# The Griffin block's two input projections as three fp32r products each, in a two-layer decoder trunk

## The chip, the core and the metric

The kernel runs on one core of one Trainium2 chip, in one launch. The metric is device time in microseconds (us), the median over several executions. One execution was also taken by the hardware profiler; its rows are shown below.

## The reference

The input x has 256 tokens (rows) of 1024 features, in float32. Two layers follow each other.

- Layer 0: RMSNorm, an input projection 1024 to 2560, a convolution branch and an attention branch, an output projection, residual add.
- Layer 1, whose mixer the change touches:

```python
def mixer_c(h, w_in, conv_w, conv_b, w_r, b_r, w_i, b_i, lam, w_out):
    u = h @ w_in
    gate, xr = jnp.split(u, 2, axis=-1)
    xr = causal_depthwise_conv(xr, conv_w) + conv_b
    y = rg_lru(xr, w_r, b_r, w_i, b_i, lam) * jax.nn.gelu(gate)
    return y @ w_out
```

  Here `w_in` is 1024 by 2048, the convolution has width 4, and `rg_lru` makes two gates r and i as sigmoids of `xr @ w_r` and `xr @ w_i` (eight blocks of 128x128 each) and runs the recurrence h_t = a_t h_(t-1) + sqrt(1 - a_t^2) i_t x_t with a = exp(-8 r softplus(-lam)).
- After each mixer: RMSNorm, then a squared-ReLU MLP (1024 to 4096 to 1024), residual add. At the end a last RMSNorm.

## The kernel before, in words

Everything stays in on-chip memory except the weights, which stream in once. Activations are held transposed: a tile has 128 features on the partitions and the 256 tokens along the free axis, so 1024 features are eight tiles `xT0` to `xT7`. A projection of one block of 128 outputs is eight matmuls (k = 0 to 7) that add up in one PSUM bank, with a 128x128 block of weights as the stationary operand and a 128x256 tile of x as the moving one. There are eight banks: `bank_a` 0 to 3 and `bank_b` 0 to 3; the projections rotate through the b banks, so the fourth one after a given one needs that one's bank read out.

**Two kinds of product.** A matmul of plain float32 operands ("whole") is one instruction in the program, which the profile records as two MATMUL rows. The MLPs instead *split* both operands into a high part, rounded to the type fp32r, and a low part, the rest, and make high*high + high*low + low*high. For the MLP's up projection `project_wide` (line 675) puts high and low of x side by side as one moving operand of 512 columns; its down projection uses three matmuls of 256 columns (`out_mm`, line 934).

**Weights.** A *piece* is 1 MB of weights, loaded by two DMAs of 512 KB on the SP queue, in the order in which `piece` (line 507) was called; a piece holds two *units* of 128 outputs each (128 rows of weights each, for the output projections). A piece lands in one of five `raw` buffers, used in rotation. `weights(u)` (line 554) splits a unit into a `wh`/`wl` pair, also in rotation, of which there are eight: for each half of the unit a cast to `wh` (on ScalarE or VectorE) and a subtraction into `wl` (on VectorE), each on 128x512 elements. From the sixth in a row on, a piece whose units stay whole lands straight in a pair (one unit in `wh`, one in `wl`), which then holds no split weights. SP issues strictly in order, and a DMA waits until its buffer has been read for the last time.

**The second mixer** (lines 1033 to 1134), with c = 0 to 7 for the blocks of 128 channels: `xr_proj(c)` projects, `xr_tail(c)` scales by `rstd` (the norm's factor, which `finish_norm` makes with one matmul of `ssum` against ones, a square root on ScalarE and a reciprocal on VectorE) and runs the width-4 convolution on VectorE; `gates(c)` makes two whole matmuls with the blocks of `w_r` and `w_i` (the piece called "ri") and two sigmoids; `recur_a`, `recur_b`, `recur_c` make the recurrence; `gate_chunk(c)` projects the gate branch, `gate_out(c)` applies GELU and multiplies. Then the output projection: `out_rows` for the first four blocks, `out_cols` for the others. The x tiles for the mixer come from `residual_chunk` (line 699), called while the first MLP's `out_cols` finishes.

**Order.** The program records all operations first, and a planner (class `Plan`) then simulates them with a table of costs and writes each engine's instructions in the order it found; matmuls keep almost the program's order. All engines run their own queue in order, and so an instruction that waits holds up those behind it. Almost all instructions carry line 310, where the planner emits them; tile names tell them apart.

Of the kernel before, what the change touches and what calls it, by code (L numbers as in the profile page):

```python
# [326 lines left out]
def hybrid_trunk(ctx, tc, x, mix_norm, mlp_norm, w_up, w_down, ab_w_in, ab_conv_w, ab_ln_g, ab_ln_b,  # L327
# [87 lines left out]
    def mms(items, after=()):  # L415

        calls, outs, ins, c = [], [], [], 0.0
        for o, l, r, st, sp in items:
            calls.append(("matmul", (o,), {"lhsT": l, "rhs": r, "start": st, "stop": sp, "skip_group_check": True}))
            outs.append(o)  # L420
            ins += [l, r]
            c += max(fsize(r) / 2400.0, 0.0533) * (1 if l.dtype == F32R else 4) + (0.0135 if l.dtype == F32R else 0.005)
        return plan.add("T", calls, outs[:1], ins, {"T": c}, after=after)
# [75 lines left out]

    pieces, units = [], []
    homes, pairs = [], {}
    turn = {"raw": 0, "pair": 0, "whole": 0}

    def piece(kind, ap, whole=True):
        n = len(pieces)
        pieces.append((kind, ap))
        us = [len(units), len(units) + 1]  # L510
        units.extend([(n, 0), (n, 1)])
        turn["whole"] = turn["whole"] + 1 if whole else 0
        if turn["whole"] > NRAW:
            i = turn["pair"] % NSPL
            turn["pair"] += 1
            homes.append((whs[i], wls[i]))
        else:
            raw = raws[turn["raw"] % NRAW]
            turn["raw"] += 1
            homes.append((raw[:, :1024], raw[:, 1024:]))  # L520
        if not whole:
            for u in us:
                pairs[u] = turn["pair"] % NSPL
                turn["pair"] += 1
        return us

    def cols(w, c, whole=True):

        return piece("c", w.rearrange("(k p) c -> p k c", p=P)[:, :, c * P:(c + 2) * P], whole)

    def rows(ap, whole=True):
        return piece("r", ap, whole)

    taken = [0, 0]
    got = {}
# [51 lines left out]
    for us in (((u_gate, 4), (u_val, 0)), ((u_q, 8), (u_k, 12))):  # L587
        for c in (0, 2):
            for u, at in us:
                u += cols(w_in, at + c)  # L590
    u_v = rows(wv[:, 0:4]) + rows(wv[:, 4:8])
    wo = ab_w_out[0].rearrange("(k p) c -> p k c", p=P)
    u_o = {}
    for k in (4, 6, 0, 2):
        u_o[k], u_o[k + 1] = rows(wo[:, k:k + 2])
    LAG, TAIL = 4, 4

    def mlp_units(layer):
        up, dn = [], []
        wd = w_down[layer].rearrange("(f p) c -> p f c", p=P)  # L600
        for f in range(0, NF + LAG, 2):
            if f < NF:
                up += cols(w_up[layer], f, False)
            if f >= LAG:
                dn += rows(wd[:, f - LAG:f - LAG + 2], False)
        return up, dn

    u_up, u_dn, u_xr, u_gt, u_co = {}, {}, [], [], []
    u_up[0], u_dn[0] = mlp_units(0)
    for c in range(0, 8, 2):  # L610
        u_xr += cols(c_w_in[0], 8 + c)
        if c == 2:
            u_r, u_i = piece("ri", None)
    for c in range(0, 8, 2):
        u_gt += cols(c_w_in[0], c)
    wco = c_w_out[0].rearrange("(k p) c -> p k c", p=P)
    for k in range(0, 8, 2):
        u_co += rows(wco[:, k:k + 2])
    u_up[1], u_dn[1] = mlp_units(1)


# [45 lines left out]
    def par(name, c):  # L667
        i = col0[name] + c
        return pcol[:, i:i + 1]


    def project(dst, u, xs):
        w = weights(u)
        for k in range(KD):
            mms([(dst, w[k], xs[k], k == 0, k == KD - 1)])

    def project_wide(b, u, xs):

# [19 lines left out]

    def residual_chunk(k, acc, gname, g0, xs):
        tt(xT[k], acc, xT[k], OP.add)  # L700
        g = par(gname, g0 + k)
        xs[k] = scaled(xT[k], g) if gname == "mix" else split_act(xT[k], g, "x", KD)
        if k in (0, KD - 2):
            act(ssum if k == 0 else sumb, xT[k], AF.Square)
        else:
            sq = rot("nsq", 2)
            act(sq, xT[k], AF.Square)
            if k < KD - 2:
                tt(ssum, ssum, sq, OP.add)
            else:  # L710
                tt(sumb, sumb, sq, OP.add)
# [219 lines left out]
        t = [bank("a") for _ in range(4)]  # L931
        return [t[c // 2][:, (c % 2) * S:(c % 2 + 1) * S] for c in range(KD)]

    def out_mm(acc, c, w, xp, start, stop):
        if not isinstance(w, tuple):
            return mms([(acc, w[c], xp, start, stop)])
        mms([(acc, a[:, c, :], b, start and n == 0, stop and n == 2)
             for n, (a, b) in enumerate(((w[0], xp[0]), (w[0], xp[1]), (w[1], xp[0])))])

    def out_rows(accs, u, xp, first):  # L940
        w = weights(u)
        for c in range(KD):
            out_mm(accs[c], c, w, xp, first and c % 2 == 0, False)

    def out_cols(accs, us, xps, done):
        ws = [weights(u) for u in us]
        for c0 in range(0, KD, 2):
            for c in (c0, c0 + 1):
                for i, (w, xp) in enumerate(zip(ws, xps)):
                    out_mm(accs[c], c, w, xp, False, i == len(us) - 1)  # L950
            done(c0)
            done(c0 + 1)

# [269 lines left out]
```

## Time and profile before

| what | us |
|---|---|
| median of 3 runs (588.99 to 589.18) | 589.08 |
| the profiled execution | 588.62 |
| its span, first to last instruction | 586.8 |
| TensorE (PE) busy | 579.9 |
| VectorE (DVE) busy | 413.1 |
| ScalarE (ACT) busy | 289.7 |

The profiled execution takes 1.8 us more than its span. In the rows below, a line gives the start, the length, the engine, then output<-inputs by the program's names without buffer numbers, the shape, and how many instructions were merged into the line; in square brackets, how long the engine sat idle before it and who ended that. Lengths of merged or pipelined instructions overlap, so the cost of one is read from the distance between starts. Matmul ends are modelled.

### The profile page before, as it was taken

How to read it: one execution, taken by the hardware profiler on the slowest of the kernel's cores; microseconds unless marked ns; L12 is line 12 of the kernel's file. 1: busy time of each engine (PE TensorE's matmuls, PEld its weight loads, DVE VectorE, ACT ScalarE, POOL GpSimd, SP SyncE). 2: the span in 40 equal slices, each digit the busy share in tenths (PEclk: the TensorE clock that was granted, in tenths of full speed). 3: DMA queues.
4: the chain of work that ended last, by engine and by line, in shares of the span. 5: the costliest groups of instructions: out<-in, count | busy, mean ns of one | idle time of the engine just before them, and what ended most of it. 6: DMA issues, size and time to landing. Idle time of an engine off the chain costs nothing.

```text
span 586.8 us, 9026 instructions
## 1 busy us (share of the span) xinstructions
PE 579.9 (99%) x3305; PEld 510.2 (87%) x3305; DVE 413.1 (70%) x946; ACT 289.7 (49%) x592; POOL 2.8 (0%) x22
## 2 busy tenths in 40 slices
PE   9999999999999999999999999999999999999995
PEld 8888768889999999999998888888888888888885
DVE  2599998599777767677446777559876767767732
ACT  4131435467554555555321798327555555545523
POOL 1000000000000000000000000000000000000000
PEclk9999999999999999999999999999999999999999
DMA  7997704125664665566677005924645664563001
GB/s 222 324 382 256 258 1 144 71 70 163 203 212 145 191 217 166 166 205 203 218 223 280 1 0 157 370 83 143 196 164 180 196 198 144 185 212 107 1 1 72
DMA packets 67612, 98.74 MB, mean 168 GB/s; under 512 B 3212, under 2 KB 55664, under 8 KB 67568
## 3 DMA queue, kind: packets, MB, share of 16 engines
q1 hardware_dynamic: 67568, 98.17, 50.7%
q8 instruction: 26, 0.43, 0.3%
q14 instruction: 18, 0.15, 0.1%
HBM read 97.11 MB, written 1.05 MB: 167 GB/s over the span
## 4 chain that ended last, share of the span: by engine, by line
PE 99%; ACT 0%; DVE 0%; issue 0%; ACTq 0%
PE bank_b L310 56%; PE bank_a L310 42%; ACT arena L395 0%; DVE arena L310 0%; ACT arena L310 0%; DVE ones L310 0%; DVE tiny L310 0%; DVE eps L310 0%; ACTq L310 0%
## 5 line engine op out<-in xcount | busy, mean ns | idle before, releaser
L310 DVE TENSOR_TENSOR wl<-raw,wh 128x512 fp32r<-128x512 f32 x256 | 175.1, 690 | 84.5 <-ACT wh L395 76.3
L395 ACT ACTIVATE wh<-raw 128x512 fp32r<-128x512 f32 x223 | 139.5, 630 | 168.2 <-PE bank_b L310 104.3
L310 PE MATMUL bank_b<-x,wh 128*128 128x512 f32 x512 | 184.7, 401 | 0.0
L310 PE MATMUL bank_b<-x,wl 128*128 128x256 f32 x512 | 143.8, 281 | 0.0
L310 PEld LDWEIGHTS bank_b<-x,wh 128*128 128x128 f32 x512 | 96.4, 188 | 20.9
L310 PEld LDWEIGHTS bank_b<-x,wl 128*128 128x128 f32 x512 | 96.8, 189 | 0.1
L310 PE MATMUL bank_a<-f,wh 128*128 128x256 f32 x512 | 93.2, 283 | 0.0
L310 PEld LDWEIGHTS bank_a<-f,wh 128*128 128x128 f32 x512 | 79.6, 191 | 1.4
L310 PE MATMUL bank_a<-f,wl 128*128 128x256 f32 x256 | 72.4, 283 | 0.0
L310 PE MATMUL bank_a<-wh,f 128*128 128x512 f32 (+1 forms) x256 | 72.2, 364 | 0.0
L310 PE MATMUL bank_b<-xg,raw 128*128 128x256 f32 x288 | 64.1, 379 | 0.0
L310 PEld LDWEIGHTS bank_b<-xg,raw 128*128 128x128 f32 x288 | 54.1, 190 | 7.3
L310 PEld LDWEIGHTS bank_a<-wh,f 128*128 128x128 f32 x256 | 45.9, 188 | 9.1
L310 DVE SCALAR_TENSOR_TENSOR arena<-arena,wcol 128x256 f32<-128x256 f32 x120 | 49.5, 478 | 0.0
L310 PEld LDWEIGHTS bank_a<-f,wl 128*128 128x128 f32 x256 | 49.0, 192 | 0.0
L310 PE MATMUL bank_a<-wl,f 128*128 128x512 f32 (+1 forms) x128 | 46.5, 363 | 0.0
L310 PE MATMUL bank_a<-arena,wh 128*128 128x256 f32 x128 | 34.4, 381 | 0.0
L310 PE MATMUL bank_a<-arena,wl 128*128 128x256 f32 x128 | 33.9, 379 | 0.0
L310 DVE TENSOR_TENSOR relu<-bank_b,relu 128x256 f32<-128x256 f32 x64 | 26.7, 417 | 10.1 <-ACT relu L310 10.1
L310 ACT ACT_TABLE_LOAD x24 | 30.8, 1283 | 3.0 <-PE bank_b L310 1.9
L310 ACT ACTIVATE relu<-relu 128x256 f32<-128x256 f32 x64 | 26.1, 411 | 8.2 <-DVE relu L310 5.1
L310 ACT ACTIVATE relu<-bank_b 128x256 f32<-128x256 f32 x64 | 23.6, 369 | 11.6 <-PE bank_b L310 11.6
(125 smaller groups left out, 594.3 us busy)
## 6 DMA issues: line engine op xcount, KB each, us to landing
raw<-in_w_up_dram SPq DMA_DIRECT2D x64, 512.0 KB, 5.7
raw<-in_w_down_dram SPq DMA_DIRECT2D x64, 512.0 KB, 4.8
raw<-in_c_w_in_dram SPq DMA_DIRECT2D x8, 512.0 KB, 5.4
raw<-in_ab_w_in_dram SPq DMA_DIRECT2D x6, 512.0 KB, 7.8
wh<-in_ab_w_in_dram SPq DMA_DIRECT2D x5, 512.0 KB, 8.7
wl<-in_ab_w_in_dram SPq DMA_DIRECT2D x5, 512.0 KB, 8.8
raw<-in_ab_w_in_dram SPq DMA_DIRECT2D x8, 256.0 KB, 5.7
wh<-in_ab_w_out_dram SPq DMA_DIRECT2D x4, 512.0 KB, 10.0
```

What stands on the lines that cost most here:

```text
L310: r.append(getattr(self.engines[o.eng], method)(*map(sub, a), **{n: sub(v) for n, v in k.items()}))
L395: return e.activation(sub(out), sub(a), AF.Copy, **({"scale": scale} if ap else {}))
```

## The change

Each call that declares a piece now says where it goes: "raw", "pair" or "split". The units of `c_w_in` (eight for the `xr` half, eight for the gate half) become "split"; the piece "ri" and the output projection's pieces are "pair". A common function `mm` makes one matmul or three, and `project` uses it (three of 256 columns each; not `project_wide`). `residual_chunk` splits x for the mixer as it does for the MLPs. The gates' matmuls and the output projection stay whole.

```diff
-    def piece(kind, ap, whole=True):
+    def piece(kind, ap, place):
...
-        turn["whole"] = turn["whole"] + 1 if whole else 0
-        if turn["whole"] > NRAW:
+        if place == "pair":
             i = turn["pair"] % NSPL
             turn["pair"] += 1
             homes.append((whs[i], wls[i]))
...
     for c in range(0, 8, 2):
-        u_xr += cols(c_w_in[0], 8 + c)
+        u_xr += cols(c_w_in[0], 8 + c, "split")
         if c == 2:
-            u_r, u_i = piece("ri", None)
+            u_r, u_i = piece("ri", None, "pair")
     for c in range(0, 8, 2):
-        u_gt += cols(c_w_in[0], c)
+        u_gt += cols(c_w_in[0], c, "split")
...
-        u_co += rows(wco[:, k:k + 2])
+        u_co += rows(wco[:, k:k + 2], "pair")
...
+    def mm(dst, w, k, x, first, last):
+
+        ps = ((w[0][:, k], x[0]), (w[0][:, k], x[1]), (w[1][:, k], x[0])) if isinstance(w, tuple) else ((w[k], x),)
+        mms([(dst, a, b, first and n == 0, last and n == len(ps) - 1) for n, (a, b) in enumerate(ps)])
+
     def project(dst, u, xs):
         w = weights(u)
         for k in range(KD):
-            mms([(dst, w[k], xs[k], k == 0, k == KD - 1)])
+            mm(dst, w, k, xs[k], k == 0, k == KD - 1)
...
-        g = par(gname, g0 + k)
-        xs[k] = scaled(xT[k], g) if gname == "mix" else split_act(xT[k], g, "x", KD)
+        xs[k] = split_act(xT[k], par(gname, g0 + k), "x", KD)
```

On PE, at the second `xr` projection of layer 1, before the change (`xg` are the scaled whole x tiles, `raw_73` holds units 0 and 1; the row with `ssum` is the norm's matmul):

```order
L310 MATMUL bank_b_109<-xg_123,raw_73 128x256
L310 MATMUL bank_b_109<-xg_124,raw_73 128x256
L310 MATMUL bank_b_110<-ssum,ones 128x256
L310 MATMUL bank_b_109<-xg_125,raw_73 128x256
L310 MATMUL bank_b_109<-xg_126,raw_73 128x256
L310 MATMUL bank_b_111<-xg_119,raw_74 128x256
```

The same place on PE after it (`x_129` to `x_136` are the split tiles of x):

```order
L310 MATMUL bank_b_108<-x_136,wh_1_509 128x256 x2
L310 MATMUL bank_b_108<-x_136,wl_1_643 128x256
L310 MATMUL bank_b_109<-x_129,wh_1_528 128x256 x2
L310 MATMUL bank_b_109<-x_129,wl_1_661 128x256
L310 MATMUL bank_b_109<-x_130,wh_1_528 128x256 x2
L310 MATMUL bank_b_109<-x_130,wl_1_661 128x256
L310 MATMUL bank_b_110<-ssum,ones 128x256
L310 MATMUL bank_b_109<-x_131,wh_1_528 128x256 x2
```

Each whole matmul became three, and the norm's matmul stands after two steps of the second projection where it stood after six.

On SP, the loads of layer 1's mixer before the change (the first digit of a name is the buffer: `wh5` is the high half of pair 5):

```order
L310 DMA raw4_75<-in_c_w_i_dram 128x8x128
L310 DMA raw0_71<-in_c_w_in_dram 128x4x256 x2
L310 DMA raw1_72<-in_c_w_in_dram 128x4x256 x2
L310 DMA wh1_2_2499<-in_c_w_in_dram 128x4x256
L310 DMA wl1_2_2505<-in_c_w_in_dram 128x4x256
L310 DMA wh2_2_2546<-in_c_w_in_dram 128x4x256
L310 DMA wl2_2_2552<-in_c_w_in_dram 128x4x256
L310 DMA wh3_2_2559<-in_c_w_in_dram 128x4x256
L310 DMA wl3_2_2568<-in_c_w_in_dram 128x4x256
L310 DMA wh4_2_2587<-in_c_w_in_dram 128x4x256
L310 DMA wl4_2_2592<-in_c_w_in_dram 128x4x256
L310 DMA wh5_2_2700<-in_c_w_out_dram 128x1024
```

And after it, from the first piece of `c_w_in` on:

```order
L310 DMA raw2_73<-in_c_w_in_dram 128x4x256 x2
L310 DMA raw3_74<-in_c_w_in_dram 128x4x256 x2
L310 DMA wh5_2_2699<-in_c_w_r_dram 128x8x128
L310 DMA wl5_2_2705<-in_c_w_i_dram 128x8x128
L310 DMA raw4_75<-in_c_w_in_dram 128x4x256 x2
L310 DMA raw0_71<-in_c_w_in_dram 128x4x256 x2
L310 DMA raw1_72<-in_c_w_in_dram 128x4x256 x2
L310 DMA raw2_73<-in_c_w_in_dram 128x4x256 x2
L310 DMA raw3_74<-in_c_w_in_dram 128x4x256 x2
L310 DMA raw4_75<-in_c_w_in_dram 128x4x256 x2
L310 DMA wh2_2_3053<-in_c_w_out_dram 128x1024
```

The piece "ri" moved from a raw buffer into pair 5, the pair in which the output projection's first piece landed; six of the eight pieces of `c_w_in` now stand behind it.

On DVE, from the end of the norm on, after the change (`bank_b0_108` holds the first `xr` projection; `raw4_75` the fifth and sixth unit of `xr`, which go to pairs 6 and 7; before it, the same rows stood there without the CAST and the `wl` rows):

```order
L310 TENSOR_TENSOR ssum_101<-ssum_101,sumb_102 128x256
L310 RECIPROCAL rstd_100<-rstd_100 128x256
L396 CAST wh6_1_805<-raw4_75 128x512
L310 TENSOR_TENSOR arena_103<-bank_b0_108,rstd_100 128x256
L310 TENSOR_TENSOR arena_103<-bank_b1_109,rstd_100 128x256
L310 TENSOR_SCALAR arena_103<-arena_103,pcol_66 128x256 x2
L310 SCALAR_TENSOR_TENSOR arena_103<-arena_103,pcol_66 128x256 x2
L310 TENSOR_TENSOR wl6_1_823<-raw4_75,wh6_1_805 128x512
L310 SCALAR_TENSOR_TENSOR arena_103<-arena_103,pcol_66 128x256 x3
L310 TENSOR_TENSOR wl6_1_823<-raw4_75,wh6_1_805 128x512
L310 SCALAR_TENSOR_TENSOR arena_103<-arena_103,pcol_66 128x256
L310 TENSOR_TENSOR arena_103<-bank_b3_111,rstd_100 128x256
```

The splits of weights now stand between the steps of the convolutions.

## Rows read from the trace of the kernel before

**Rows 1.** The page, busy time of TensorE and its weight loads; chain that ended last.

```profile
PE 579.9 (99%) x3305; PEld 510.2 (87%) x3305; DVE 413.1 (70%) x946; ACT 289.7 (49%) x592; POOL 2.8 (0%) x22
...
PE 99%; ACT 0%; DVE 0%; issue 0%; ACTq 0%
```

**Rows 2.** Busy by stretch: length, PE, PEld, DVE, ACT, POOL, granted clock, DMA, GB/s.

```profile
314.60:347.00 32.40, 32.40 (x152) 28.49 (x151) 27.40 (x66) 21.79 (x35) 0.00 (x0) 1.00 0.13 50
...
307.50:370.10 62.60, 62.60 (x293) 55.06 (x292) 43.92 (x105) 42.67 (x72) 0.00 (x0) 1.00 0.35 123
```

**Rows 3.** Timeline of PE, the second mixer from its start to its output projection.

```profile
307.47 6.21 PE L310 MATMUL bank_b<-xg,raw 128*128 128x256 f32 x28
313.51 0.59 PE L310 MATMUL bank_b<-ssum,ones 128*128 128x256 f32 x2
313.95 11.39 PE L310 MATMUL bank_b<-xg,raw 128*128 128x256 f32 x52
...
370.07 3.62 PE L310 MATMUL bank_a<-arena,wh 128*128 128x256 f32 x16
```

**Rows 4.** Timeline of PE, the first MLP's last down products; thirty such triples.

```profile
295.95 0.40 PE L310 MATMUL bank_a<-f,wh 128*128 128x256 f32 x2
...
306.75 0.40 PE L310 MATMUL bank_a<-f,wh 128*128 128x256 f32 x2
```

**Rows 5.** The page's costliest groups: down products' weight loads, and ScalarE's table loads.

```profile
L310 PEld LDWEIGHTS bank_a<-f,wh 128*128 128x128 f32 x512 | 79.6, 191 | 1.4
...
L310 ACT ACT_TABLE_LOAD x24 | 30.8, 1283 | 3.0 <-PE bank_b L310 1.9
```

**Rows 6.** Timeline of DVE, norm and convolutions, and a pair of weight splits.

```profile
314.65 1.75 DVE L310 RECIPROCAL rstd<-rstd 128x256 f32<-128x256 f32 x1 [4.49 <-ACT rstd L310]
...
317.19 0.73 DVE L310 TENSOR_SCALAR arena<-arena,pcol 128x256 f32<-128x256 f32 x2
317.83 2.46 DVE L310 SCALAR_TENSOR_TENSOR arena<-arena,pcol 128x256 f32<-128x256 f32 x6
320.20 0.42 DVE L310 TENSOR_TENSOR arena<-bank_b,rstd 128x256 f32<-128x256 f32 x1
...
367.76 1.29 DVE L310 TENSOR_TENSOR wl<-raw,wh 128x512 fp32r<-128x512 f32 x2 [0.75 <-ACT wh L395]
368.97 0.42 DVE L310 TENSOR_TENSOR arena<-bank_b,rstd 128x256 f32<-128x256 f32 x1
```

**Rows 7.** Timeline of SP: first load into pair 5, and second MLP's first loads.

```profile
306.46 0.34 SPq L310 DMA_DIRECT2D wh<-in_c_w_out_dram  x1
...
358.65 7.16 SPq L310 DMA_DIRECT2D raw<-in_w_up_dram  x6
```

**Rows 8.** Busy by stretch, columns as Rows 2, just after SP's burst began.

```profile
308.00:310.00 2.00, 2.00 (x11) 1.77 (x10) 1.47 (x5) 1.12 (x3) 0.00 (x0) 1.00 0.96 383
```

**Rows 9.** Timeline of ACT: casts of the second MLP's first weights, waiting for DMA.

```profile
364.50 1.15 ACT L395 ACTIVATE wh<-raw 128x512 fp32r<-128x512 f32 x2 [1.68 <-DMA raw<-in_w_up_dram]
...
367.10 1.15 ACT L395 ACTIVATE wh<-raw 128x512 fp32r<-128x512 f32 x2 [1.15 <-DMA raw<-in_w_up_dram]
```

**Rows 10.** Timeline of DVE where the second MLP starts: its last x tiles.

```profile
397.95 0.76 DVE L310 TENSOR_TENSOR xT<-bank_a,xT 128x256 f32<-128x256 f32 x2
398.62 0.68 DVE L310 TENSOR_TENSOR wl<-raw,wh 128x512 fp32r<-128x512 f32 x1
399.22 0.88 DVE L310 SCALAR_TENSOR_TENSOR x<-xT,pcol,x 128x256 fp32r<-128x256 f32 x2
```

**Rows 11.** Timeline of PE at the same place, the first split projection.

```profile
397.98 0.28 PE L310 MATMUL bank_b<-x,wl 128*128 128x256 f32 x1
398.10 0.40 PE L310 MATMUL bank_b<-x,wh 128*128 128x512 f32 x1
398.33 0.28 PE L310 MATMUL bank_b<-x,wl 128*128 128x256 f32 x1
...
399.83 0.39 PE L310 MATMUL bank_b<-x,wh 128*128 128x512 f32 x1
```

More of the change, by code (lines that the diff above doesn't have):

```diff
@@ L504, in hybrid_trunk @@
     homes, pairs = [], {}
-    turn = {"raw": 0, "pair": 0, "whole": 0}
-    def piece(kind, ap, whole=True):
+    turn = {"raw": 0, "pair": 0}
+    def piece(kind, ap, place):
         n = len(pieces)
@@ L520, in piece @@
             homes.append((raw[:, :1024], raw[:, 1024:]))
-        if not whole:
+        if place == "split":
             for u in us:
@@ L525, in piece, with cols, rows @@
         return us
[L527 to L532, printed above, removed]
+    def cols(w, c, place):
+        return piece("c", w.rearrange("(k p) c -> p k c", p=P)[:, :, c * P:(c + 2) * P], place)
+    def rows(ap, place):
+        return piece("r", ap, place)
     taken = [0, 0]
@@ L589, in hybrid_trunk @@
             for u, at in us:
-                u += cols(w_in, at + c)
-    u_v = rows(wv[:, 0:4]) + rows(wv[:, 4:8])
+                u += cols(w_in, at + c, "raw" if len(pieces) < NRAW else "pair")
+    u_v = rows(wv[:, 0:4], "pair") + rows(wv[:, 4:8], "pair")
     wo = ab_w_out[0].rearrange("(k p) c -> p k c", p=P)
@@ L594, in hybrid_trunk @@
     for k in (4, 6, 0, 2):
-        u_o[k], u_o[k + 1] = rows(wo[:, k:k + 2])
+        u_o[k], u_o[k + 1] = rows(wo[:, k:k + 2], "pair")
     LAG, TAIL = 4, 4
@@ L602, in mlp_units @@
             if f < NF:
-                up += cols(w_up[layer], f, False)
+                up += cols(w_up[layer], f, "split")
             if f >= LAG:
-                dn += rows(wd[:, f - LAG:f - LAG + 2], False)
+                dn += rows(wd[:, f - LAG:f - LAG + 2], "split")
         return up, dn
@@ L932, in accumulators @@
         return [t[c // 2][:, (c % 2) * S:(c % 2 + 1) * S] for c in range(KD)]
[L934 to L938, printed above, removed]
     def out_rows(accs, u, xp, first):
@@ L942, in out_rows @@
         for c in range(KD):
-            out_mm(accs[c], c, w, xp, first and c % 2 == 0, False)
+            mm(accs[c], w, c, xp, first and c % 2 == 0, False)
     def out_cols(accs, us, xps, done):
@@ L949, in out_cols @@
                 for i, (w, xp) in enumerate(zip(ws, xps)):
-                    out_mm(accs[c], c, w, xp, False, i == len(us) - 1)
+                    mm(accs[c], w, c, xp, False, i == len(us) - 1)
             done(c0)
```

## The prediction, made before the result was known

> **What bounds the kernel now.** I read the page first: TensorE is busy for 579.9 of 586.8 us and owns 99% of the chain that ended last [rows 1]. A busy TensorE may still hide waits, because its ends are modelled, so I went on to its timeline and read distances between starts. From the first projection of the second mixer at 307.47 to its output projection at 370.07 there is no irregular distance [rows 3]: 28 records, which the order shows to be 14 whole matmuls, take 313.51 - 307.47 = 6.04 us, 0.4314 us each; the 62.60 us of the stage divided by that are 145.1, and the program has 128 projection matmuls, 16 gate matmuls and the norm's, 145. So TensorE never waits there, and every microsecond taken from it counts as long as no other engine falls behind. Busy time by stretch tells who could: in these 62.6 us VectorE works for 43.9 and ScalarE for 42.7; between 314.6 and 347.0, where the convolutions run, VectorE already has 27.4 of 32.4 [rows 2].
>
> **What the change removes and adds on TensorE.** Out go 16 units times 8 steps, 128 whole matmuls at 0.4314 us. In come three products of 128x256 each with fp32r operands. The same form runs in the first MLP's down products: thirty triples from 295.95 to 306.75, 10.80 us, so 0.360 us a triple and 0.120 us a product [rows 4]. There too the second product reuses the weights of the first and loads them again. The sum: 128 x (0.4314 - 0.360) = **9.14 us less**. The Trainium skill, TensorE: Matmul & The Clock Gate, section Back-to-back issue gap, puts a warm matmul of N columns at N/2.4 + 2.5 ns, so 109 ns at 256 columns. By that estimate three would take 0.328 us and the gain would be 13.3 us. Our rows show 0.120 us, and the sum goes by them. The granted clock is 1.00 throughout the stage, the 2.4 GHz level [rows 2]; TensorE is not to go idle, so I leave it there.
>
> **What it adds elsewhere, and what hides it.** Each of the 16 units is now split: two casts and two subtractions. The subtractions are VectorE's, 1.21 us for a pair, 0.605 each [rows 6]; 32 of them are 19.4 us. Of 32 casts the order gives four to VectorE and 28 to ScalarE, where two take about 1.05 us from start to start [rows 9]. Eight more scalar_tensor_tensor of the x split are 3 us on VectorE. I take nothing of this onto the path, for four reasons, each of them a race that I worked out with TensorE's new pace (2.88 us a unit) from 307.47.
>
> *First, x itself.* The first unit's last steps need the last x tiles. The second MLP starts in the same way: sums at 397.95, a weight split in between, both low halves done by 400.1; TensorE takes step 6 at 399.83, on its regular beat of 0.35 us [rows 10, 11]. The mixer's chain has no weight split in between, and asks at nearly the same pace. Cost 0.
>
> *Second, the piece "ri".* It now lands in pair 5, free only when the first MLP's last products have read it. Before, the first load into that pair went out at 306.46 [rows 7]; "ri" takes that place, and the pieces of units 4 to 7 of `xr` and all of the gate half, which were not held up by pair 5 before, queue behind it. Unit 4's first half is the third DMA of this burst, issued near 307.4. In the burst before the second MLP a first load issued at 358.65 released its cast at 364.50, a later one at 367.10 [rows 7, 9]: 5.9 to 8.5 us. So it lands between 313.3 and 315.9; by volume (three times 0.52 MB at 383 GB/s [rows 8] from 308) nearer the early end. I take 314.5. On VectorE the cast of this unit is queued ahead of everything in `xr_tail`. Reciprocal: its start followed the norm's matmul by 314.65 - 313.51 = 1.14 us and it lasts 1.75 [rows 3, 6]; the matmul now stands at 307.47 + 2.88 + 0.72 = 311.07, so `rstd` is there at 313.96, and the cast waits 0.5 us for its data. Bank b0 is then read by 315.3; `xr` unit 3 wants that bank at 316.5. Unit 4's low halves are ready at 317.6 and 319.4, wanted at 319.4 and 320.9. Margins of 1.2 to 1.8 us; cost 0.
>
> *Third, VectorE in the convolutions.* From that cast to the end of the last convolution (which `gates(7)` reads) the order has one cast, 9 tensor_tensor, 8 tensor_scalar, 24 scalar_tensor_tensor and 17 subtractions. Distances: 0.335 us for a tensor_tensor, (398.62 - 397.95)/2 [rows 10], and the same for the cast; 0.32 us, (317.83 - 317.19)/2, for a tensor_scalar and 0.395 us, (320.20 - 317.83)/6, for a scalar_tensor_tensor [rows 6]. Sum 0.34 + 3.02 + 2.56 + 9.48 + 10.29 = 25.7 us, so 340.2. TensorE reaches `gates(7)` after eight `xr` units, the norm, 14 gate matmuls and two gate-half units: 307.47 + 10 x 2.88 + 15 x 0.4314 = 342.7. Margin 2.5 us. Next comes the tightest place: gate-half unit 3 is split into pair 5, which `gates(7)` itself frees at 343.6. Ahead of its second subtraction and with it stand four tensor_tensor, two scalar_tensor_tensor, a cast and six subtractions, 6.1 us, so its halves are ready at 345.7 and 346.3; TensorE wants them at 346.7 and 347.9. Margins 1.0 and 1.6 us; cost 0.
>
> *Fourth, ScalarE.* About 22 casts fall into the stage, 11.6 us; the order has 13 table loads where 15 stood, at 1.28 us each [rows 5], 2.6 us less. So 42.7 becomes some 52 of the new 53.4 us. Nearly full, but with late deadlines: what comes last, GELU of blocks 4 to 7, is wanted only by `out_cols`, after 32 whole matmuls of the output projection, 13.8 us after the stage. Its tightest early point is the sigmoids of `gates(4)`, whose bank gate-half unit 1 reuses: adding its rows up I find 338.1 against 339.9. Cost 0.
>
> The output projection's weights go out as the gate half's pairs come free, from 338 on, over 20 us ahead of need. The second MLP's first loads still wait for the recurrence to release the arena, near 358 as before [rows 7], while its first products move from 397.98 [rows 11] to 388.8; a split followed ten microseconds behind those loads, at 367.76 [rows 6], so 20 us of cover are left.
>
> **The sum.** The profiled execution took 588.62 us: 588.62 - 9.14 = 579.48. The median of the runs is 0.46 us above that execution, so **579.9 us**.
>
> **The rivals.**
>
> *A, VectorE (or ScalarE) is late:* the chain of 25.7 + 6.1 us is made of distances in smooth stretches. If its steps cost their full spans, 0.68 for a subtraction (1.29 less 0.605) and 0.485 for a scalar_tensor_tensor (2.46 less five times 0.395) [rows 6], 23 times 0.08 and 26 times 0.09 add 4.2 us. The margin at unit 3 eats 1.0, so TensorE waits 3.2 us: 583.1. Half of that excess gives 581.0. For it: nearly no idle time is left on VectorE for 32 us. Against it: the splits separate steps that depend on each other.
>
> *B, "ri" and unit 4 land late:* at 315.9 the whole VectorE chain shifts by 1.4 us; bank b0 is read 0.2 us late, and gate-half unit 3 comes another 0.2 us late: 580.3. At 10 us after issue, 317.4, the bank costs 1.7 us and unit 3 again 0.2: 581.8.
>
> *C, slower than before:* weight loads. The new form has three loads where a whole matmul, with two records, has two, and a load is busy for 191 ns [rows 5]. If loads did not run beside products, a product would cost more. By the beat of 512 and 256 columns, 0.23 and 0.12 us [rows 11], a column is 0.43 ns, so 128 columns of weights add 0.055 us: 0.175 a product, 0.525 a step, 128 x 0.094 = 12.0 us more, 601.1. It decides from 0.144 us a product on. Against it stands 0.120 us over ninety products, each with its own load [rows 4]. The Trainium skill's page TensorE: Matmul & The Clock Gate, section The mechanism, says that a weight load overlaps running matmuls only when the row group differs; all of ours use all rows. By that rule C would hold; this trace does not agree, with 0.120 us.
>
> That the change does not do what it says is excluded by the order, which has the 384 products.
>
> **Chances.** The forecast, within 0.5 us of 579.9: 0.75. A: 0.13. B: 0.08. C: 0.02. Something unseen that costs more than 2 us: 0.02. The lower bound is a product at 0.118 us, 0.8 us less: 579.1; the upper takes in B and half of A, 581.9; what lies above is 0.1 or a little more. A measurement of this kernel can tell about 0.2%, 1.2 us, from no change. Faster by more: 0.96; within: 0.02; slower: 0.02.
>
> **What would show it.** Right: TensorE from the first `xr` matmul to the output projection in 53.4 us with triples of 0.36, no idle before it. Wrong: a gap ahead of `xr` unit 3 or 4 with a DMA of `c_w_in` behind the VectorE cast (B); gaps ahead of `gates(6)`, `gates(7)` or gate-half unit 3, released by VectorE (A); triples longer than 0.36 with no wait (C).

## The result, and the profile after it

| what | us |
|---|---|
| median before, beside it (4 runs, 588.99 to 589.18) | 589.05 |
| median after (4 runs, 579.59 to 581.4) | 580.83 |
| ratio, 95% interval | 0.9857, 0.9840 to 0.9874 |
| the profiled execution after, and its span | 581.11, 579.3 |

The kernel became 8.2 us faster; forecast were 9.1 us and 579.9. The gain is clear of noise, the interval ends well below 1, and it is a little short: the median lies 0.9 us above the forecast, outside the 0.5 us that had been given a chance of 0.75, and inside the range of 579.1 to 581.9. Where the shortfall lies is read in the same views as before. The page of the changed kernel, TensorE's busy time and the chain that ended last (before: [rows 1]):

```profile
PE 571.0 (99%) x3433; PEld 507.6 (88%) x3433; DVE 434.0 (75%) x989; ACT 302.5 (52%) x619; POOL 2.7 (0%) x22
PE 91%; DMA 4%; ACT 3%; DVE 1%; issue 1%; SPq 0%; ACTq 0%
```

The chain is no longer TensorE's alone: 9% of it now runs through others, DMA and ScalarE above all. Busy time of the stage from the first product of the second mixer to its output projection (columns as in [rows 2]):

```profile
307.77:362.70 54.93, 53.93 (x420) 52.46 (x419) 50.21 (x118) 45.07 (x79) 0.00 (x0) 1.00 0.67 218
```

62.60 us have become 54.93, 7.67 less; 53.4 were forecast. DVE rose from 43.92 to 50.21 and ACT from 42.67 to 45.07. TensorE's timeline shows both the new pace and the 1.5 us that are missing (before: [rows 3]):

```profile
307.77 0.40 PE L310 MATMUL bank_b<-x,wh 128*128 128x256 f32 x2
...
308.14 0.40 PE L310 MATMUL bank_b<-x,wh 128*128 128x256 f32 x2
...
311.38 0.59 PE L310 MATMUL bank_b<-ssum,ones 128*128 128x256 f32 x2
...
339.73 0.59 PE L310 MATMUL bank_b<-arena,wl 128*128 128x256 f32 x2
341.18 0.50 PE L310 MATMUL bank_b<-x,wh 128*128 128x256 f32 x2 [0.85 <-ACT arena L310]
341.52 0.28 PE L310 MATMUL bank_b<-x,wl 128*128 128x256 f32 x1
...
347.89 0.40 PE L310 MATMUL bank_b<-x,wh 128*128 128x256 f32 x2
348.44 0.39 PE L310 MATMUL bank_b<-x,wl 128*128 128x256 f32 x1 [0.15 <-DVE wl L310]
...
362.70 3.62 PE L310 MATMUL bank_a<-arena,wh 128*128 128x256 f32 x16
```

Steps follow each other at 0.36 us (307.77, 308.14), as in the down products of [rows 4], and the norm's matmul stands at 311.38, 3.61 us after the first product (forecast 3.60). Two rows carry a wait. The gate matmul at 339.73, the last one ahead of gate-half unit 1, takes 0.43 us, so the first low product of gate-half unit 1 was due at 340.16 + 0.24 = 340.40; it came at 341.52, **1.1 us late**, because ScalarE's sigmoids of `gates(4)` still held the bank. In gate-half unit 3 the low product due at 347.89 + 0.24 = 348.13 came at 348.44, **0.3 us late**, behind a subtraction of VectorE.

VectorE's timeline at the two ends of the convolutions (before: [rows 6]):

```profile
312.51 1.75 DVE L310 RECIPROCAL rstd<-rstd 128x256 f32<-128x256 f32 x1 [1.81 <-ACT rstd L310]
315.52 0.43 DVE L396 CAST wh<-raw 128x512 fp32r<-128x512 f32 x1 [1.25 <-DMA raw<-in_c_w_in_dram]
315.87 0.75 DVE L310 TENSOR_TENSOR arena<-bank_b,rstd 128x256 f32<-128x256 f32 x2
...
340.98 0.48 DVE L310 SCALAR_TENSOR_TENSOR arena<-arena,pcol 128x256 f32<-128x256 f32 x1
...
346.13 0.68 DVE L310 TENSOR_TENSOR wl<-raw,wh 128x512 fp32r<-128x512 f32 x1
347.70 0.69 DVE L310 TENSOR_TENSOR wl<-raw,wh 128x512 fp32r<-128x512 f32 x1 [0.89 <-ACT wh L395]
```

The cast at 315.52 waited 1.25 us for weights (forecast: 314.5, a wait of 0.5). The last step of the convolutions ends near 341.4, 25.9 us after that cast began; the chain had been costed at 25.7 from the same rows.

ScalarE's timeline (`arena<-bank_b,pcol` are the gates' sigmoids, `wh<-raw` the casts):

```profile
315.52 0.63 ACT L395 ACTIVATE wh<-raw 128x512 fp32r<-128x512 f32 x1 [3.04 <-DMA raw<-in_c_w_in_dram]
317.33 1.15 ACT L395 ACTIVATE wh<-raw 128x512 fp32r<-128x512 f32 x2 [1.17 <-DMA raw<-in_c_w_in_dram]
...
329.36 0.63 ACT L395 ACTIVATE wh<-raw 128x512 fp32r<-128x512 f32 x1 [0.41 <-DMA raw<-in_c_w_in_dram]
...
337.17 1.28 ACT L310 ACT_TABLE_LOAD   x1
338.46 0.51 ACT L310 ACTIVATE arena<-arena 128x256 f32<-128x256 f32 x1
338.99 1.28 ACT L310 ACT_TABLE_LOAD   x1
340.29 0.84 ACT L310 ACTIVATE arena<-bank_b,pcol 128x256 f32<-128x256 f32 x2
...
347.05 0.61 ACT L395 ACTIVATE wh<-raw 128x512 fp32r<-128x512 f32 x1
```

From 315.52 on ScalarE has no idle time except behind loads of `c_w_in`. The sigmoids of `gates(4)` end at 340.29 + 0.84 = 341.13; 338.1 was forecast. SP's timeline says why the weights were late (before: [rows 7]):

```profile
306.77 0.37 SPq L310 DMA_DIRECT2D wh<-in_c_w_r_dram  x1
307.23 1.59 SPq L310 DMA_DIRECT2D wl<-in_c_w_i_dram  x1
308.88 4.36 SPq L310 DMA_DIRECT2D raw<-in_c_w_in_dram  x4
```

"ri" went out 1.0 us before the first product, as forecast, but its second half kept SP for 1.59 us, and the load of `xr` unit 4 followed at 308.88, not near 307.4 (plus 0.3 us, by which this execution reached the stage later than the one of before). The chain of waits joins the pieces; a row of SP's timeline stands below it:

```profile
308.88 6.62 DMA raw<-in_c_w_in_dram
...
318.05 0.60 DVE wl L310
...
318.81 10.47 DMA raw<-in_c_w_in_dram
...
329.36 0.63 ACT wh L395
```

```profile
317.50 1.21 SPq L310 DMA_DIRECT2D raw<-in_c_w_in_dram  x1
```

A load (6.62 us) holds VectorE's cast; another one lands at 329.3 and holds ScalarE's cast at 329.36; and behind this cast, in order, stand the sigmoids that TensorE waits for. The chain also puts VectorE's subtraction at 318.05 ahead of the issue of that second load, as if a raw buffer had come free too late. The other rows do not bear this link out: the subtraction ended at 318.65, when SP was still busy with the issue before (317.50 + 1.21 = 318.71), and from 316 to 330 the loads came without a pause, at 347 to 375 GB/s in each stretch of 2 us. So the load of 329.3 was late together with the whole stream of loads.

### The profile page after: what moved, and what is told of

Read it like the earlier page. It is cut to its first block, busy times and chain, and to the rows that moved or that the text cites. A ratio compares the mean times of both kernels' runs of the same rounds, so it can differ in the third digit from the quotient of the medians.

```text
span 579.3 us, 9374 instructions
## 1 busy us (share of the span) xinstructions
PE 571.0 (99%) x3433; PEld 507.6 (88%) x3433; DVE 434.0 (75%) x989; ACT 302.5 (52%) x619; POOL 2.7 (0%) x22
## 4 chain that ended last, share of the span: by engine, by line
PE 91%; DMA 4%; ACT 3%; DVE 1%; issue 1%; SPq 0%; ACTq 0%
PE bank_b L310 49%; PE bank_a L310 42%; DMA raw<-in_c_w_in_dram 3%; ACT arena L310 1%; ACT L310 1%; DMA arena<-in_x_dram 1%; ACT wh L395 1%; SPq L310 0%; DVE arena L310 0%; DVE wl L310 0%; ACT arena L395 0%; DVE tiny L310 0%; ACTq L395 0%; DVE wh L396 0%; ACTq L310 0%
## 5 line engine op out<-in xcount | busy, mean ns | idle before, releaser
L310 DVE TENSOR_TENSOR wl<-raw,wh 128x512 fp32r<-128x512 f32 x288 | 196.3, 689 | 82.3 <-ACT wh L395 78.9
L395 ACT ACTIVATE wh<-raw 128x512 fp32r<-128x512 f32 x252 | 156.7, 629 | 170.9 <-PE bank_b L310 108.0
L310 PE MATMUL bank_b<-x,wh 128*128 128x512 f32 (+1 forms) x768 | 232.2, 363 | 0.8 <-ACT arena L310 0.8
L310 PE MATMUL bank_b<-x,wl 128*128 128x256 f32 x640 | 180.3, 282 | 0.2 <-DVE wl L310 0.2
L310 PEld LDWEIGHTS bank_b<-x,wh 128*128 128x128 f32 x768 | 136.8, 190 | 22.3 <-ACT arena L310 1.2
L310 PEld LDWEIGHTS bank_b<-x,wl 128*128 128x128 f32 x640 | 121.6, 190 | 0.5 <-DVE wl L310 0.4
L310 PE MATMUL bank_b<-xg,raw 128*128 128x256 f32 x160 | 35.8, 380 | 0.0
L310 PEld LDWEIGHTS bank_b<-xg,raw 128*128 128x128 f32 x160 | 29.9, 190 | 4.0 <-DVE arena L310 0.2
L310 DVE SCALAR_TENSOR_TENSOR relu<-relu,rstd 128x256 f32<-128x256 f32 x64 | 26.8, 424 | 1.8
```

The lines of the kernel that those rows point to most:

```text
L310: r.append(getattr(self.engines[o.eng], method)(*map(sub, a), **{n: sub(v) for n, v in k.items()}))
L395: return e.activation(sub(out), sub(a), AF.Copy, **({"scale": scale} if ap else {}))
```

## The experiments

Times are medians; "before" was run beside each group: 589.13 us for the first four, 588.77, 588.99 and 589.03 for the next three groups. "Stage" is always the time from the first product of the second mixer to its output projection in the profiled execution, "landing" the start of the first cast that waited for the load of `xr` unit 4, counted from that first product, as are the sigmoids of the last column; all in us. The recorded expectations set a queue theory (late loads hold up engines that work in order) against a capacity theory (ScalarE has too much to do in the stage, whenever the loads land). Line numbers in rows shift with the edits.

| kernel | median (range) | ratio, interval | stage | landing | first sigmoid of gates(4) |
|---|---|---|---|---|---|
| changed, first profile | 580.83 (579.59 to 581.4) | 0.9857, 0.9840 to 0.9874 | 54.93 | 7.75 | 32.52 |
| changed, second | 580.76 (580.66 to 581.73) | 0.9862, 0.9848 to 0.9875 | 54.63 | 7.85 | 32.22 |
| changed, third | 580.94 (580.0 to 581.52) | 0.9862, 0.9847 to 0.9876 | 53.38 | 7.01 | 30.97 |
| one Exp moved | 580.65 (580.09 to 581.0) | 0.9855, 0.9842 to 0.9869 | 54.62 | 8.11 | 28.80 |
| Exp grouped | 580.07 (579.79 to 580.63) | 0.985, 0.9837 to 0.9863 | 54.12 | 7.91 | 28.74 |
| Exp grouped, cast later | 580.08 (579.88 to 580.27) | 0.9849, 0.9835 to 0.9864 | 54.03 | 7.56 | 28.58 |
| cast later | 580.74 (580.36 to 580.78) | 0.9858, 0.9842 to 0.9875 | 53.97 | 7.60 | 31.54 |
| cast later, again | 580.61 (580.33 to 581.42) | 0.986, 0.9843 to 0.9876 | 54.39 | 7.88 | 31.97 |
| 1 MB more behind "ri" | 584.17 (583.79 to 584.25) | 0.9915, 0.9901 to 0.9928 | 57.78 | 11.05 | 34.92 |
| "ri" in its own buffer | 579.76 (579.69 to 580.36) | 0.9845, 0.9831 to 0.9858 | 53.40 | no wait | 28.94 |
| "ri" in the old x tiles, planned anew | 579.58 (579.38 to 579.71) | 0.984, 0.9827 to 0.9854 | 53.40 | no wait | 29.87 |
| planned with later landings | 579.52 (579.31 to 579.96) | 0.9842, 0.9829 to 0.9856 | 53.39 | 7.65 | 29.80 |
| only the xr half split | 584.58 (583.64 to 584.85) | 0.9924, 0.9912 to 0.9936 | 58.00 | 7.68 | 29.86 |

**The changed kernel again.** 

> The changed kernel once more, for the spread of its runs (579.59 to 581.4 us so far) and a second trace. Queue theory: the stage from the first xr product to the output projection takes 53.4 us of products plus a wait ahead of gate-half unit 1 that follows the landing of the c_w_in loads, so it differs between runs (0 to 2 us) while everything else is the same to 0.3 us; median 580.0 to 581.2. Capacity theory (ScalarE has too much to do in the stage, whenever the loads land): the wait is 1.1 us again, within 0.2.

The same two waits, 54.63 us: the shortfall is no accident of one execution. The wait at gate-half unit 1 was 0.8 us, within what the queue theory allows and a little under the 0.9 to 1.3 of the capacity theory; by itself this run decides nothing. (A third profile, further down, came out otherwise.)

**One Exp moved.** The planner's finished order is edited: one Exp activation of the recurrence, which stood between two table loads ahead of the sigmoids of `gates(4)`, goes behind them on ScalarE.

```diff
...
+        last = sig[-7 + 0]
+        exp = max(i for i in acts if i < last and order[i][0].func == AF.Exp)
...
+        return kept + moved + order[last + 1:]
```

> One exponential of the recurrence (block 1) is moved behind the two sigmoids of gates(4) on ScalarE; every other engine's order is untouched. It stood between two table loads, 3.1 us in all, ahead of those sigmoids. Queue theory: the sigmoids end 3 us earlier, the wait of 1.1 us ahead of gate-half unit 1 is gone, the 0.3 us inside gate-half unit 3 may stay; stage 53.5 to 53.8 us, median 579.5 to 580.0. Capacity theory: the work is the same, so the wait turns up at the next bank (gate-half unit 2 or 3); stage 54.6 to 55.0 us, median within 0.3 of the changed kernel.

The sigmoids came at 28.80, 3.4 to 3.7 us earlier, and the wait at gate-half unit 1 was gone. Two stood at gate-half unit 3 in its place (TensorE's timeline):

```profile
347.16 0.50 PE L327 MATMUL bank_b<-x,wh 128*128 128x256 f32 x2 [0.49 <-ACT wh L412]
347.88 0.39 PE L327 MATMUL bank_b<-x,wl 128*128 128x256 f32 x1 [0.22 <-DVE wl L327]
```

Now TensorE waited for ScalarE's cast itself. The stage did not change: 54.62 us is what the capacity theory had forecast, and the 53.5 to 53.8 of the queue theory missed. Moving one instruction in a queue that is behind only chose which consumer pays; the next two runs decide between the theories.

**"ri" in a buffer of its own.** The tiles of x that the first mixer has left free take it, so SP need not wait for pair 5. Every engine keeps its order.

```diff
...
+        if form == 2 and shared[name] in ("wh5", "wl5"):
+            return (xgs, 1024 * (shared[name] == "wl5"))
...
```

> The piece ri goes to a buffer of its own (the first layer's x tiles, free by then); the order of all instructions on all engines stays, so SP no longer waits for pair 5 and the c_w_in pieces are loaded from about 272 us on. Queue theory: no cast of c_w_in waits for a DMA, both waits of TensorE are gone; stage 53.4 us, median 579.4 to 579.8, spread under 0.4 us. Capacity theory: the wait ahead of gate-half unit 1 stays at about 1 us; median 580.5 to 581.

Busy time of the stage by engine (columns as in [rows 2]):

```profile
307.70:361.10 53.40, 53.40 (x421) 52.48 (x420) 50.69 (x121) 46.42 (x83) 0.00 (x0) 1.00 0.33 115
```

No row of TensorE carries a wait in the stage, and none of ScalarE waits for `c_w_in`. ScalarE does the same work and is busy for 46.42 us of 53.40, VectorE for 50.69. So neither engine is too slow for the stage, the capacity theory falls, and the two waits are gone together with the late loads. (Pair 5 is free earlier here as well, but that is not what ended them: in the changed kernel the casts into it, at 345.46 on VectorE and 347.05 on ScalarE, had no idle time ahead of them.) The five executions spread over 0.67 us, where under 0.4 was expected.

**More load behind "ri".** Eight loads of 128 KB that nothing reads follow "ri" on SP; the rest keeps its order.

```diff
...
+                for q in range(4):
+                    nc.sync.dma_start(pools["xg"][0][4 * j + q].rearrange("p (k c) -> p k c", k=2), w[0][2 * q:2 * q + 2].rearrange("h i j -> i h j"))
```

> Behind ri eight loads of 128 KB into the same free tiles are added, 1 MB, with the order of all other instructions as it is. Queue theory: the c_w_in pieces land 3 to 4 us later, the cast at the head of VectorE's queue holds bank b0, so a wait of 1 to 3 us appears ahead of xr unit 3, and the one ahead of gate-half unit 1 stays at 0.5 to 2 us; stage 56 to 59 us, median 582.5 to 585. Capacity theory: ScalarE's own work is what counts, so later loads cost less than 1 us more.

The load of unit 4 landed 3.3 us later than in the changed kernel's first profile, and the stage took 2.85 us more, 4.4 more than without any wait. TensorE's timeline, its stage by stretch (columns as in [rows 2]), and VectorE's timeline:

```profile
316.39 0.28 PE L310 MATMUL bank_b<-x,wl 128*128 128x256 f32 x1
319.30 0.80 PE L310 MATMUL bank_b<-x,wh 128*128 128x256 f32 x2 [2.63 <-DVE arena L310]
...
320.11 0.63 PE L310 MATMUL bank_b<-x,wh 128*128 128x256 f32 x2
...
323.06 0.40 PE L310 MATMUL bank_b<-x,wh 128*128 128x256 f32 x2
```

```profile
319.30:321.00 1.70, 1.70 (x8) 1.70 (x9) 1.70 (x6) 1.07 (x2) 0.00 (x0) 0.51 1.09 366
...
323.00:325.00 2.00, 2.00 (x19) 2.00 (x19) 2.00 (x6) 1.60 (x3) 0.00 (x0) 1.00 1.10 349
```

```profile
318.49 0.43 DVE L398 CAST wh<-raw 128x512 fp32r<-128x512 f32 x1 [4.56 <-DMA raw<-in_c_w_in_dram]
```

The wait moved to where rival B had put it: `xr` unit 3 waits for bank b0, which VectorE reads only after the cast. Its first product was due at 316.39 + 0.12 = 316.51 and came 2.8 us late. The other 1.6 us are the clock's: after the idle time the granted clock was 0.51, the 1.2 GHz level, and six steps took 3.76 us, 319.30 to 323.06, instead of 2.16; from 323 on it was 1.00 again. In the changed kernel's first profile, with idle times of 0.85 and 0.15 us, it stayed at 1.00. The wait of 0.5 to 2 us that the queue theory still had at gate-half unit 1 was not there: TensorE, 4.4 us behind, wanted that bank only at 344.2, and the sigmoids ended at 342.36 + 0.84 = 343.20.

**Exp grouped.** Two lone Exp activations now run with the group of three behind the sigmoids of `gates(5)` and `gates(6)`; two table loads fall away. Nothing else moves on any engine. Against the run with one Exp moved:

```diff
-        last = sig[-7 + 0]
-        exp = max(i for i in acts if i < last and order[i][0].func == AF.Exp)
+        last = sig[-3]
+        exp = max(i for i in acts if i < sig[-8] and order[i][0].func == AF.Exp)
```

> Everything as in the changed kernel, the late loads too, but the two Exp activations that ScalarE runs one by one around the sigmoids of gates(4) now run with the three that follow the sigmoids of gates(5) and gates(6). Two table loads, 2.57 us of ScalarE's work, fall away; nothing else moves on any engine. Theory (late casts cost time only because ScalarE, with nearly as much work as the stage is long, cannot catch up): with 2.57 us of work less it catches up, both waits vanish, the stage from the first x product to the output projection takes 53.4 to 53.7 us, about 579.8 us in all. First rival (the late landing costs by itself, whatever ScalarE has to do): the wait behind the weights of gate-half unit 3 stays, stage near 54.6, 580.7 us. Second rival (VectorE waits for the Exp results that now come later, and hands the lateness on): a new wait behind VectorE, stage over 54.6 us.

The first wait vanished and the second stayed: the stage took 54.12 us where the theory had 53.4 to 53.7 and its first rival 54.6, in part a miss. TensorE's and VectorE's timelines of this run:

```profile
346.28 0.40 PE L327 MATMUL bank_b<-x,wh 128*128 128x256 f32 x2
347.14 0.39 PE L327 MATMUL bank_b<-x,wl 128*128 128x256 f32 x1 [0.46 <-DVE wl L327]
```

```profile
345.12 0.43 DVE L413 CAST wh<-raw 128x512 fp32r<-128x512 f32 x1
...
345.79 1.29 DVE L327 TENSOR_TENSOR wl<-raw,wh 128x512 fp32r<-128x512 f32 x2
```

ScalarE's cast was ready (344.17 to 344.79), but VectorE did the second of the two subtractions only from 346.4 to 347.0, and TensorE's low product, due at 346.28 + 0.24 = 346.52, came at 347.14. VectorE had waited for nothing since its 1.4 us behind the late load. So lateness reaches TensorE by a second queue, VectorE's.

**The cast on VectorE moved, with and without the grouping.** The cast that waits for unit 4's weights goes behind the first convolution steps, right ahead of the subtraction that needs it. VectorE's order, as a diff:

```diff
 RECIPROCAL rstd<-rstd 128x256
-CAST wh_1_805<-raw_75 128x512
 TENSOR_TENSOR arena<-bank_b_108,rstd 128x256
 TENSOR_TENSOR arena<-bank_b_109,rstd 128x256
 TENSOR_SCALAR arena<-arena,pcol 128x256 x2
 SCALAR_TENSOR_TENSOR arena<-arena,pcol 128x256 x2
+CAST wh_1_805<-raw_75 128x512
 TENSOR_TENSOR wl_1_823<-raw_75,wh_1_805 128x512
```

> The kernel with the grouped Exp activations, and besides it one cast on VectorE, the one that waited 1.4 us for the late weights of xr unit 4, stands four kinds of rows later, right ahead of the first subtraction that needs it. The late loads stay. Theory as amended after the run with the grouped Exp (the late landing reaches TensorE by two queues, ScalarE's at gate-half unit 1 and VectorE's at gate-half unit 3, each without idle time to make the delay good): the wait of 0.5 us that was left at gate-half unit 3 vanishes too, and the stage takes 53.4 to 53.5 us, 579.7 us in all. Rival (gate-half unit 3 is late because its pair comes free late, whatever VectorE did before): the wait stays, stage near 54.1 us, 580.1 us.

> The changed kernel with only that cast on VectorE moved back; ScalarE's order, its table loads and the late loads stay. Amended theory: VectorE no longer waits for the load and runs about 1.2 us earlier, but ScalarE still reaches the sigmoids of gates(4) late, so the wait of about 1.1 us at gate-half unit 1 stays: stage 54.5 to 54.9 us, 580.7 us. Rival (all of the loss comes by VectorE's queue): no waits, stage 53.4 us, 579.7 us.

With the grouping the wait stayed (0.4 us), a miss: 54.03 and 580.08 us are what the rival had forecast. VectorE no longer waited for the load, but its timeline has another wait:

```profile
342.88 0.43 DVE L335 TENSOR_TENSOR arena<-arena 128x256 f32<-128x256 f32 x1 [1.01 <-ACT arena L335]
```

The grouped Exp now come too late for VectorE, 1.0 us; the grouping takes back what the cast gave. The time thus does not tell the theory from its rival, but the rows speak against the rival's cause, a pair that comes free late: in this run `gates(7)` is through with the pair at 343.30 + 0.43 = 343.73, and the casts into it start at 344.49 on ScalarE and 345.36 on VectorE, behind other work and with no idle time ahead of them. Without the grouping no row with a wait was left at gate-half unit 1, against both theories (54.5 to 54.9 and 53.4), and the stage took 53.97 us. It was run again beside the changed kernel:

> The same kernel as the run with only the cast on VectorE moved back, beside the changed kernel on one chip, since in the first run the stage was 53.97 us, shorter than expected, but it began late and the time did not move. Theory of a loop (VectorE's wait for the late load also delays the subtraction that frees a raw buffer, with it a later load, and so ScalarE's casts): the wait at gate-half unit 1 is gone again and the stage takes 53.8 to 54.1 us, so the median is 0.5 to 0.9 us below that of the changed kernel beside it. Rival (the first profile was one of a kind): stage 54.5 to 54.9 us, equal medians.

> The changed kernel once more, for comparison beside it: stage 54.6 to 54.9 us, a wait of about 1.1 us at gate-half unit 1 and one at gate-half unit 3, 580.7 us.

TensorE's two rows with a wait in the second run with the cast moved:

```profile
340.78 0.50 PE L318 MATMUL bank_b<-x,wh 128*128 128x256 f32 x2 [0.31 <-ACT arena L318]
348.05 0.39 PE L318 MATMUL bank_b<-x,wl 128*128 128x256 f32 x1 [0.16 <-DVE wl L318]
```

This time a wait of 0.3 us was left there, and the stage of 54.39 us lies between the forecasts of the loop (53.8 to 54.1) and of its rival. The loop is not shown. ScalarE's DMA wait near 329, 0.41 us in the changed kernel's first profile, is under 0.1 us in these two runs, but it is 0.24 with the cast moved and the Exp grouped, and there is none where one Exp was moved and the cast stood in its old place. SP's issue of that load took 1.82 us in the first profile and 1.82 with the cast moved and the Exp grouped, although VectorE's subtraction came earlier there. What the move is worth in time, 0 to 0.3 us by the medians, is inside their ranges and stays open.

The changed kernel beside it gave the most telling profile of all. Its timelines of SP and of VectorE, and its chain of waits:

```profile
307.19 0.37 SPq L310 DMA_DIRECT2D wh<-in_c_w_r_dram  x1
307.65 0.53 SPq L310 DMA_DIRECT2D wl<-in_c_w_i_dram  x1
308.24 16.38 SPq L310 DMA_DIRECT2D raw<-in_c_w_in_dram  x12
```

```profile
312.94 1.75 DVE L310 RECIPROCAL rstd<-rstd 128x256 f32<-128x256 f32 x1 [1.81 <-ACT rstd L310]
315.20 0.43 DVE L396 CAST wh<-raw 128x512 fp32r<-128x512 f32 x1 [0.52 <-DMA raw<-in_c_w_in_dram]
```

```profile
299.96 8.40 PE bank_a L310 x70
308.36 53.38 PE bank_b L310 x418
...
```

Here SP needed 0.53 us for the second half of "ri", the load of unit 4 went out at 308.24 and landed 7.01 us after the first product (forecast 7.03), VectorE waited 0.52 us (forecast 0.5), and TensorE did not wait at all: 53.38 us, where 54.6 to 54.9 had been expected. The same program with an earlier landing, and the prediction's 53.4 to the tenth. This execution took 580.0 us, 0.7 of which is a wait for the first mixer's weights at the start of the program, long before the change.

**Planned with later landings, and "ri" elsewhere.** The planner's DMA costs are set to what the trace shows, or "ri" gets the old x tiles and the order is planned anew.

```diff
-DMA_START, DMA_DONE, DMA_RATE = 1.7, 1.0, 360e3
+DMA_START, DMA_DONE, DMA_RATE = 1.7, 3.0, 340e3
```

```diff
...
-            u_r, u_i = piece("ri", None, "pair")
+            u_r, u_i = piece("ri", None, "raw")
+            homes[-1] = ("xg", "xg")
+            turn["raw"] -= 1
```

> The changed kernel, planned with a DMA that completes 2 us later and runs at 340 instead of 360 KB per us, as the trace of the changed kernel shows late landings; the loads and where they land stay, the order on ScalarE and VectorE changes: sigmoids now stand ahead of casts whose weights come late, and single Exp activations are fewer. Theory: no wait at gate-half unit 1 or 3, a stage of 53.4 to 53.8 us, about 579.8 us, unless the new order, which reaches from the first instruction to the last, loses elsewhere. Rival (the landing costs by itself): stage 54.6 us or more, 580.7 us.

> The changed kernel with the piece of w_r and w_i in the eight tiles of x that the first mixer has left free, and the order planned anew around it. Theory: like the run with the piece in a buffer of its own, a stage of 53.4 us and 579.7 to 579.9 us: nothing is left to win in this stage but TensorE's own products. Rival (the planner finds more elsewhere, or loses it): over 0.5 us away from that.

Busy time of the stage by engine in the first of the two:

```profile
307.65:361.04 53.39, 53.39 (x421) 52.47 (x420) 50.56 (x118) 44.84 (x83) 0.00 (x0) 1.00 0.76 242
```

Both have no wait and the stage at its floor. The first is the more instructive: its loads land as late as ever (7.65), but the cast that waited on VectorE is on ScalarE now, and the sigmoids stand ahead of casts that are not urgent. Their ratios to the kernel before, 0.9842 and 0.984, against 0.9857 to 0.9862 for the changed kernel, are about 1 us less; the intervals overlap, and the changed kernel's third profile had the same stage. Of the changed kernel's twelve timed executions two lie below 580.4 us, of the fourteen of these two kernels and of the one with "ri" in its own buffer all do. The ranges of these three overlap, so none of them is the fastest.

**Only the xr half.** The gate half is whole again; nothing of the computation is left out, x is kept in both forms.

```diff
-        u_gt += cols(c_w_in[0], c, "split")
+        u_gt += cols(c_w_in[0], c, "pair")
...
```

> Only the eight xr units are split; the gate half is whole again, its weights land in pairs, and x is kept in both forms (eight scaled copies more). By the sum, half of the 128 steps keep their 0.4314 us: 64 x 0.0714 = 4.57 us more than three products everywhere, so a stage of 53.42 + 4.57 = 57.99 us without a wait. Theory (lateness plus a full ScalarE): the gate half's casts are gone from ScalarE, so there is no backlog and no wait at gate-half unit 1 or 3: 58.0 to 58.3 us, 584.3 us in all. Rival (the piece of w_r and w_i behind pair 5 costs its 1.2 us in any case): 59.2 us, 585.5.

The stage is 58.00 us against 57.99 worked out, without a wait, though "ri" is as late as in the changed kernel: without the gate half's casts ScalarE has made the delay good by 324.27, where it waits 1.25 us for TensorE.

## Why the prediction was right, and where it was not

**The sum held.** 128 steps at 0.360 instead of 0.4314 us: where nothing waits the stage takes 53.38 to 53.40 us in four profiles, 9.2 us less than the 62.60 of before, and half of the change gives half of it (58.00). The rate was taken from another place in the trace, where the same form of instruction already ran, and no better estimate was needed. The Trainium skill, TensorE: Matmul & The Clock Gate, section Back-to-back issue gap, gives the formula from which the prediction estimated 109 ns a product and 13.3 us for an isolated matmul; for a stream of matmuls that each have a weight load it gives about 81 ns at 128 columns and 131 ns at 512. The 0.120 us a product measured here, at 256 columns, lies between these two and does not agree with 109 ns. Weight loads stayed hidden: PEld is busy for 52.46 us of the stage and costs nothing, and rival C falls.

**First** (x) held: the first eight steps, 307.77 to 310.65, are regular.

**Second** ("ri" and unit 4) is where the mistake begins. The bounds were right: from the first product, 313.3 to 315.9 less 307.47 is 5.8 to 8.4 us, and ten profiles gave 7.0 to 8.1. The point taken, "I take 314.5", was the earliest of what occurs. Two parts of it were too small: SP's issue of the second half (1.33 to 1.84 us in nine of ten profiles, 0.53 in one; the run with more load is not counted) and the pace of the burst, 1.37 us a load by the 383 GB/s of [rows 8], where casts came every 1.52 us (in the third profile of the changed kernel the first came at 315.20 and the seventh at 324.30).

**Third** (VectorE) was right in its length, 25.9 against 25.7 us, but had no room for the wait ahead of it. And a half was mistaken: the first half of gate-half unit 3 is cast by ScalarE and subtracted second (the subtraction at 347.70 waits for ScalarE's cast, and TensorE's low product for that subtraction), so the margin there was 346.7 less 346.3, 0.4 us, not 1.0.

**Fourth** (ScalarE), "338.1 against 339.9. Cost 0", is the step that failed. With the load on time the sigmoids end 31.8 us after the first product (30.97 + 0.84), wanted at 32.4: the margin was 0.6 us, not 1.8. The burst's slower pace, six loads at 0.15 us, accounts for 0.9 of the 1.2 us if the forecast counted 1.37 us a load; its adding up is not on record. With the usual landing it is gone: 0.74 us later in the first profile, 0.3 more at the next load (317.33, 1.81 us behind the first instead of 1.52), 0.4 more at the cast of 329.36, and the sigmoids start at 32.52 instead of 30.97. Of these 1.55 us the margin takes 0.6, and TensorE lost the rest, 1.1 with rounding and the hand-over. That ScalarE would be busy for some 52 us was wrong too; 45 to 46 were measured. The first profile has the 22 casts, but five casts were already among the 42.7 us of before; it has 12 table loads, not 13, and six activations of the recurrence fewer in the stage (25 after 31). It is not short of time over the stage, as "ri" in its own buffer shows; it is short of time to make good a delay, because behind the late load it has no idle time of its own up to 363 that it could give.

**The rivals.** What happened is the cause of B (late loads by way of pair 5) with the effect of A (gaps behind ScalarE and VectorE at the gate half). B had priced a landing at 315.9 at 0.4 us, by bank b0 and unit 3 alone; the first profile's landing, 315.2 on the prediction's clock (307.47 + 7.75), cost 1.5. None of the prediction's signs named the larger wait, at gate-half unit 1 behind ScalarE. That 580.83 us lies in the range is in part luck: its upper end had been made of B's bank and A's longer steps, and in the changed kernel neither occurred (no wait at bank b0; 25.9 us for 25.7). The later landing of the run with 1 MB more went B's own way, to bank b0, and by B's arithmetic: 4.0 us behind 314.5 (307.47 + 11.05 = 318.5) the bank is read 2.8 us late, and 2.8 were measured. The 1.6 us of the lower clock behind it are in none of the prediction's terms.

Shown by runs: that the loss comes with the landing and goes with it (own buffer; one program with both landings), and that order alone can absorb it (planned with later landings). Not shown: why SP's second issue takes 0.5 us once and 1.3 to 1.8 us otherwise, and that VectorE's late subtraction delays a later load.

## What to carry to other kernels

Price the change on the bound engine by rows of the same instruction elsewhere in the trace; this is good to a tenth. Price the margins of the other engines not at one landing time but at the late end of what loads do, and follow a late load through every in-order queue that it holds, to the banks and tiles that TensorE wants from the work behind it. A wait of TensorE can cost more than its length: 2.8 us of lateness cost 4.4 here, because the granted clock fell after it. Where a small piece shares a buffer with work that ends late, everything behind it on the DMA queue is late as well; a spare buffer, or an order that keeps urgent work ahead of waiting casts, gave back about 1 us here.

## What the runs showed of the hardware that was not expected

- The issue of one 512 KB load on SP took 0.37 us when it was the first of the burst, and 1.33 to 1.84 us for the second in nine profiles of ten; in the tenth the second took 0.53 and the third 1.75. Before the change one issue of eight in the same place took 1.36.
- A run of 512 KB loads landed one every 1.52 us, 345 GB/s. The Trainium skill, DMA: Bandwidth & Descriptors, section Specifications, gives about 358 GB/s as what one core gets from HBM; an estimate from that figure is 1.46 us a load, and the trace is within 4% of it. The 383 GB/s of [rows 8], read in the first 2 us of a burst, were not kept up.
- After 2.63 us without a product the granted clock of TensorE was 0.51, the 1.2 GHz level, and a step of three products took 0.64 us instead of 0.36 (run with 1 MB more).
- Up to the stage the profiled executions of these kernels differ by 1.1 us (first product at 307.28 to 308.40, those planned anew left aside), so differences of less than 1 us between medians of four runs are read better from the stage than from the total.
